# A weight load cut by partitions: three down-weight transfers of a routed expert layer issued as 112 + 8 + 8 partitions

## The chip, the cores and the metric

The kernel runs on one core of a Trainium2 chip. The metric is the device time of one launch in microseconds. The kernel before takes 1207.47 us, the median of three runs (1206.26 to 1207.69). One further execution was profiled; all rows of a trace below come from it.

## The reference, cut to what matters

One decoder layer over 256 tokens of width 1024: a layer norm, two token mixers, then an expert layer with 32 experts of which each token uses four. Only the expert layer touches the change. Each expert has up weights of 1024 x 2048 floats (8 MB) and down weights of 1024 x 1024 floats (4 MB).

```python
def expert_block(args):
    e, tok = args
    xe = x[tok]
    gu = xe @ w_up[e] + b_up[e]
    g = jnp.minimum(gu[:, :F], SWIGLU_LIMIT)
    u = jnp.clip(gu[:, F:], -SWIGLU_LIMIT, SWIGLU_LIMIT)
    act = (u + 1.0) * (g * jax.nn.sigmoid(SWIGLU_ALPHA * g))
    return act @ w_down[e] + b_down[e]
```

The results are weighted by the router's gates, added up per token, added to the residual and normalised again.

## The kernel before

The first part of the kernel (up to about 320 us) does the mixers and the router. After it the experts are worked through one after another, at 32 *positions*: position 0 to 31 is an order of the experts that is found at run time from the number of tokens each one has. All experts' weights have to be read from HBM, 384 MB in all.

Weights live in a ring of five buffers, `R[0]` to `R[4]`, of 128 partitions x 32 KB (4 MB) each. In the order listing they are R_67 to R_70 and R_1960. A position needs three buffers' worth: the first half of the up weights ("a"), the second half ("b") and the down weights ("d"). For positions 5 to 29 (`WHOLE`, line 28) one transfer fills a whole buffer; positions 30 and 31 and the early ones are loaded in halves of 2 MB, and the very last half is cut into four pieces of 128 partitions x 4 KB (lines 208 to 210).

`load_next` (line 177) issues one load on SyncE's queue as soon as a buffer is released. `free(p, k)` calls it right behind the last matmul that reads a half buffer. The list `order` (line 167) says what is loaded next: a, b of a position, and the down weights of the position before between them. The address of an expert is read into a register first (line 190).

In a down load, `src` is the expert's down matrix seen as 128 partitions x 2 halves x 4096 floats, that is, two runs of 16 KB for each partition, and `to` is the same shape in the ring. Each load completes on one of eight semaphores (DMAHW0 to DMAHW7 in the order listing), which are used in turn. Every engine that takes part in a load ends its share with a packet of 4 bytes to that semaphore. Behind position 17's up weights `load_row` (line 843) also loads one row of 4 KB into a single partition, issued at 796.84 us.

`step` (line 957) is the work of a position on TensorE: `up_part` for the up matmuls (line 703) and `down_half` for the down matmuls (line 730). The first matmul that reads a buffer waits for its load. TensorE's order of work around the change is written out by hand (`steps`, line 159, and the loop at line 1097). Behind position 31 come the scatter (line 745), the statistics (lines 1131 to 1137), a loop over left-over tokens that has nothing to do in this run (line 1154), the last normalisation (lines 1200 and 1204) and the stores (line 1205).

Of the kernel before, what the change touches and what calls it, by code (L numbers as in the profile page):

```python
# [27 lines left out]
WHOLE = range(5, 30)  # L28
LEFT_AT, RESIDUAL_AT, NORM_AT = 5, (7, 12), 17
W0, W1, W2, W3, W4, W5 = 9, 3, 9, 7, 5, 3  # L30
MS = {mybir.EngineType.PE}
STARTS = {mybir.EngineType.PE, mybir.EngineType.DVE, mybir.EngineType.Activation}

# [21 lines left out]
def tile_kernel(ctx: ExitStack, tc: tile.TileContext, x, ln_in_g, ln_in_b, w_in, gmlp_ln_g, gmlp_ln_b,  # L55
                w_spatial, b_spatial, w_branch_a, w_branch_b, w_out, ln_mix_g, ln_mix_b, w_router,
                b_router, w_up, b_up, w_down, b_down, ln_ffn_g, ln_ffn_b, out):
    nc = tc.nc
# [7 lines left out]
    def ps_mm():  # L66
        return bank["pool"].tile([P, 512], FT, name="mm", bufs=bank["mm"])
# [104 lines left out]
    def half(slot):  # L172
        return R[slot // 2][:, slot % 2 * 4096:slot % 2 * 4096 + 4096]
# [3 lines left out]
    def load_next(slot):  # L177
        done.append(slot)
        if len(ring) == len(order):
            return  # L180
        p, k = order[len(ring)]
        n = 2 if p in WHOLE else 1
        if len(done) < n:
            return
        slots = done[-n:]
        done.clear()
        for i, to in enumerate(slots):
            ring[p, k[0] + str(int(k[1]) + i)] = to
        if p not in expert_at:
            expert_at[p] = nc.values_load(dyn["ids"][0:1, p:p + 1], engines=[mybir.EngineType.SP], min_val=0,  # L190
                                          max_val=NE - 1)
        e, h = expert_at[p], int(k[1])
        if n == 2:
            assert h == 0 and slots[0] % 2 == 0 and slots[1] == slots[0] + 1
            to = R[slots[0] // 2]
        else:
            to = half(slot)
        if k[0] == "d":
            src = wd[e] if isinstance(e, int) else wd[bass.ds(e, 1)].rearrange("o p h n -> (o p) h n")
            if n == 2:  # L200
                to = to.rearrange("p (h n) -> p h n", h=2)
            else:
                src = src[:, h]
        else:
            src = wu[e] if isinstance(e, int) else wu[bass.ds(e, 1)].rearrange("o p n -> (o p) n")
            lo = 8192 * (k[0] == "b") + 4096 * h
            src = src[:, lo:lo + 4096 * n]
        if len(ring) == len(order):
            for j in range(4):
                nc.sync.dma_start(to[:, j * 1024:(j + 1) * 1024], src[:, j * 1024:(j + 1) * 1024])  # L210
        else:
            nc.sync.dma_start(to, src)

# [352 lines left out]
    for i in range(n_pieces):  # L566
# [29 lines left out]
        if nm == "A" and hf == 1:  # L596
            attend()
            for slot in (4, 5, 6, 7):
                load_next(slot)
        if nm == "B":  # L600
            to_T(G1, hTh, hTl, (hf,))
        if i >= n_pieces - 3:
            for slot in ((2, 3), (0,), (1,))[i - n_pieces + 3]:
                load_next(slot)
# [30 lines left out]
    sp2 = ctx.enter_context(tc.tile_pool(name="s2", bufs=1, reuse_waits="tile"))  # L635
    R.append(sp2.tile([P, 8192], FT, name="R4"))
    load_next(8)
    load_next(9)
    hT2 = sp2.tile([P, NC, 2 * GRP * CAP], FT, name="hT2")
# [439 lines left out]

    with tc.manual_schedule(engines=MS):  # L1080
        def free(p, k):
            load_next(ring[p, k])
# [71 lines left out]
    with tc.For_i(0, n_left) as i:  # L1154
# [27 lines left out]
        for j in range(2):  # L1182
            to = [ps_mm(), ps_mm()]
# [51 lines left out]
```

## Time and profile before

| | us |
|---|---|
| median of three runs | 1207.47 |
| lowest, highest | 1206.26, 1207.69 |
| the profiled execution | 1209.77 |
| its span, first to last instruction | 1208.0 |
| TensorE busy in the span | 1111.3 |
| VectorE busy | 414.3 |
| ScalarE busy | 214.8 |
| GpSimd busy | 110.9 |
| moved by DMA | 451.06 MB |

The profiled execution lies 2.3 us above the median, and 1.8 us of it lie outside the span. Times on the rows count from the span's start. The core has 16 DMA engines that carry all transfers; "DMA share" is how busy they are on average, so that 0.50 may be eight engines working and eight with nothing left. A transfer is split over the engines in packets, here one for each contiguous run.

### The profile page before, as it was taken

How to read it: one execution, taken by the hardware profiler on the slowest of the kernel's cores; microseconds unless marked ns; L12 is line 12 of the kernel's file. 1: busy time of each engine (PE TensorE's matmuls, PEld its weight loads, DVE VectorE, ACT ScalarE, POOL GpSimd, SP SyncE). 2: the span in 40 equal slices, each digit the busy share in tenths (PEclk: the TensorE clock that was granted, in tenths of full speed). 3: DMA queues.
4: the chain of work that ended last, by engine and by line, in shares of the span. 5: the costliest groups of instructions: out<-in, count | busy, mean ns of one | idle time of the engine just before them, and what ended most of it. 6: DMA issues, size and time to landing. Idle time of an engine off the chain costs nothing. (4 is left out here: it accounts for less than half of the span.)

```text
span 1208.0 us, 21799 instructions
## 1 busy us (share of the span) xinstructions
PE 1111.3 (92%) x9725; PEld 581.6 (48%) x9725; DVE 414.3 (34%) x787; ACT 214.8 (18%) x355; POOL 110.9 (9%) x121
## 2 busy tenths in 40 slices
PE   8999999999899889889999998999999899999793
PEld 6787888874444244343444343434333434344331
DVE  7964645564413123113122231413222221222213
ACT  5445643422101001010000010101010100010010
POOL 2800200000000001001000000100010010100000
PEclk8999999999999889788999999899999999999886
DMA  9554548667899999999999999999999999999993
GB/s 350 196 209 159 223 175 312 245 261 296 356 430 431 430 430 432 436 425 432 426 435 430 431 434 429 428 399 431 431 432 431 432 431 431 430 431 429 428 429 132
DMA packets 44208, 451.06 MB, mean 373 GB/s; under 512 B 2968, under 2 KB 3628, under 8 KB 26064
## 3 DMA queue, kind: packets, MB, share of 16 engines
q1 hardware_dynamic: 43504, 449.47, 88.8%
q8 instruction: 78, 1.28, 0.4%
q10 hardware_dynamic: 608, 0.16, 0.1%
q14 instruction: 18, 0.15, 0.0%
HBM read 448.58 MB, written 1.05 MB: 372 GB/s over the span
## 5 line engine op out<-in xcount | busy, mean ns | idle before, releaser
L703 PE MATMUL mm<-R,hT 128*32 128x512 f32 x3136 | 374.8, 603 | 5.3 <-DMA R<-in_w_up_dram 5.3
L730 PE MATMUL at<-R,actT 128*32 128x256 f32 x3328 | 222.6, 410 | 19.9 <-DMA R<-in_w_down_dram 10.8
L703 PEld LDWEIGHTS mm<-R,hT 128*32 128x32 f32 x3136 | 89.1, 110 | 185.0 <-issue 171.0
L709 DVE TENSOR_SCALAR gg<-mm 64x512 f32<-64x512 f32 x49 | 33.5, 683 | 380.2 <-PE mm L703 380.1
L730 PEld LDWEIGHTS at<-R,actT 128*32 128x32 f32 x3328 | 102.5, 116 | 116.0 <-issue 35.0
L712 POOL TENSOR_TENSOR gg<-gg,sg 64x512 f32<-64x512 f32 x52 | 66.0, 1270 | 842.0 <-ACT sg L710 842.0
L480 DVE TENSOR_TENSOR wlo<-R,whi 128x1024 fp32r<-128x1024 f32 x80 | 112.2, 1415 | 77.6 <-ACT whi L472 77.2
L530 PE MATMUL mm<-whi,hTh 128*128 128x512 f32 x256 | 100.7, 401 | 0.8 <-ACT R L489 0.8
L530 PE MATMUL mm<-wlo,hTh 128*128 128x512 f32 x256 | 99.9, 398 | 0.3 <-DVE wlo L480 0.3
L530 PE MATMUL mm<-whi,hTl 128*128 128x512 f32 x256 | 99.9, 398 | 0.0
L472 ACT ACTIVATE whi<-R 128x1024 fp32r<-128x1024 f32 x80 | 84.3, 1056 | 86.8 <-PE mm L530 80.9
L710 ACT ACTIVATE sg<-gg 64x512 f32<-64x512 f32 x52 | 32.8, 631 | 282.5 <-DVE gg L709 260.4
L737 ACT ACTIVATE y<-at 128x256 f32<-128x256 f32 x52 | 20.0, 384 | 342.5 <-PE at L730 342.5
L662 PEld LDWEIGHTS tp<-pt,xn 128*128 128x128 f32 x448 | 57.6, 201 | 29.5 <-DVE hT L667 18.8
L662 PE MATMUL tp<-pt,xn 128*128 128x128 f32 (+2 forms) x448 | 67.4, 296 | 0.0
L745 PE MATMUL ac<-y,qt 32*128 32x256 f32 x832 | 61.5, 410 | 0.5 <-ACT y L737 0.5
L670 ACT ACTIVATE hT<-tp,lm 128x128 f32<-128x128 f32 (+2 forms) x56 | 24.9, 444 | 182.2 <-PE tp L662 182.2
L745 PEld LDWEIGHTS ac<-y,qt 32*128 32x128 f32 x832 | 38.6, 189 | 37.6 <-issue 34.8
L722 DVE COPY actT<-tp 128x256 f32<-128x256 f32 x52 | 22.1, 425 | 95.3 <-PE tp L720 95.2
L720 PEld LDWEIGHTS tp<-ident,act 64*128 64x128 f32 x208 | 28.8, 209 | 54.0 <-issue 18.7
L530 PEld LDWEIGHTS mm<-wlo,hTh 128*128 128x128 f32 x256 | 48.0, 188 | 12.6 <-DVE wlo L480 1.4
L530 PEld LDWEIGHTS mm<-whi,hTh 128*128 128x128 f32 x256 | 48.2, 189 | 11.9 <-ACT R L489 0.9
(273 smaller groups left out, 844.8 us busy)
## 6 DMA issues: line engine op xcount, KB each, us to landing
R<-in_w_up_dram SPq DMA_DIRECT2D x50, 4096.0 KB, 29.3
R<-in_w_down_dram SPq DMA_DIRECT2D x25, 4096.0 KB, 29.1
R<-in_w_up_dram SPq DMA_DIRECT2D x28, 2048.0 KB, 11.5
R<-in_w_in_dram SPq DMA_DIRECT2D x13, 2048.0 KB, 11.7
R<-in_w_down_dram SPq DMA_DIRECT2D x13, 2048.0 KB, 33.0
R<-in_w_branch_a_dram SPq DMA_DIRECT2D x2, 2048.0 KB
R<-in_w_branch_b_dram SPq DMA_DIRECT2D x2, 2048.0 KB, 8.8
R<-in_w_out_dram SPq DMA_DIRECT2D x2, 2048.0 KB
```

The costliest lines, as they stand in the source:

```text
L472: nc.scalar.activation(hi, w, AF.Copy)
L480: nc.vector.tensor_tensor(lo, w, hi.bitcast(FT), op=OP.subtract)
L530: nc.tensor.matmul(ps[t], (a_l if k == 1 else a_h)[:, c, t * P:(t + 1) * P], (lo if k == 2 else hi)[:, cc], start=c == 0 and k == 0, stop= ...
L662: nc.tensor.matmul(ps[:, i * w:(i + 1) * w], zn[:, t, c * P:(c + 1) * P], pt[:, t, :w], start=t == 0, stop=t == T - 1)
L670: nc.scalar.activation(dst[:, c, :w], ps[:, i * w:(i + 1) * w], AF.Identity, scale=lm[:, 0, c:c + 1], bias=lm[:, 1, c:c + 1])
L703: nc.tensor.matmul(ps[n * CAP:(n + 1) * CAP], xs[:, c], w[:, o:o + 512], start=False, stop=c == NC - 1)
L709: nc.vector.tensor_scalar(gg, ps[:2 * CAP], LIMIT, None, op0=OP.min)
L710: nc.scalar.activation(sg, gg, AF.Sigmoid, scale=SW_ALPHA)
L712: nc.gpsimd.tensor_tensor(gg, gg, sg, op=OP.mult)
L720: nc.tensor.transpose(ps[:, c * 2 * CAP:(c + 1) * 2 * CAP], v[:, c], ident[:2 * CAP, :2 * CAP])
L730: nc.tensor.matmul(py[n * CAP:(n + 1) * CAP, :256], at[:, c, h], w[:, o:o + 256], start=h == 0 and c == 0, stop=h == 1 and c == 3)
L745: nc.tensor.matmul(to[n // 2][:, n % 2, t * 256:(t + 1) * 256], qt[s, t], y[s], start=start and t == 0, stop=stop and t == T - 1)
```

## The change

At positions 27, 28 and 29 the down load of 128 partitions becomes three loads on the same queue, one behind another: partitions 0 to 111, 112 to 119 and 120 to 127. The bytes, their places and their order are the same.

```diff
+EIGHTHS = (27, 28, 29)
...
         if len(ring) == len(order):
             for j in range(4):
                 nc.sync.dma_start(to[:, j * 1024:(j + 1) * 1024], src[:, j * 1024:(j + 1) * 1024])
+        elif k[0] == "d" and p in EIGHTHS:
+            for lo, hi in ((0, 112), (112, 120), (120, 128)):
+                nc.sync.dma_start(to[lo:hi], src[lo:hi])
         else:
             nc.sync.dma_start(to, src)
```

SyncE's queue at position 29, before: the down load into R_1960, then the two halves of position 30's "b". The brackets name the semaphores that an issue waits for; PE is TensorE's.

```order
L212 DMA R_1960<-in_w_down_dram 128x2x4096 [waits DMAHW7_49,PE_49]
L212 ISA
L212 DMA R_70<-in_w_up_dram 128x4096 [waits DMAHW0_49,PE_49]
L212 ISA
L212 DMA R_70<-in_w_up_dram 128x4096 [waits PE_49]
```

The same place with the change (line 212 is now 214 or 216):

```order
L214 DMA R_1960<-in_w_down_dram 112x2x4096 [waits DMAHW1_49,PE_49]
L214 ISA
L214 DMA R_1960<-in_w_down_dram 8x2x4096 [waits DMAHW2_49]
L214 ISA
L214 DMA R_1960<-in_w_down_dram 8x2x4096 [waits DMAHW3_49]
L216 ISA
L216 DMA R_70<-in_w_up_dram 128x4096 [waits DMAHW4_49,PE_49]
L216 ISA
L216 DMA R_70<-in_w_up_dram 128x4096 [waits DMAHW5_49,PE_49]
```

Two issues were added, each with its own semaphore and a wait for the load that used that semaphore last; what follows stands two places later in the queue and completes on other semaphores.

TensorE's queue at the down matmuls of position 29 (two blocks of tokens, 64 matmuls), up to the first up matmul of position 30's "b"; before:

```order
L685 MATMUL tp<-ident,ptg 128x128
L730 MATMUL at<-R_1960,actT 32x256 [waits DMAHW5_49]
L730 MATMUL at<-R_1960,actT 32x256 x31
L730 MATMUL at<-R_1960,actT 32x256 [waits Activation_49]
L730 MATMUL at<-R_1960,actT 32x256 x15
L745 MATMUL ac<-y,qt 128x256 x8
L730 MATMUL at<-R_1960,actT 32x256 x16
L703 MATMUL mm<-R_70,hT_1963 32x512 [waits DMAHW6_49]
```

With the change:

```order
L689 MATMUL tp<-ident,ptg 128x128
L734 MATMUL at<-R_1960,actT 32x256 [waits DMAHW3_49,DMAHW2_49,DMAHW1_49]
L734 MATMUL at<-R_1960,actT 32x256 x31
L734 MATMUL at<-R_1960,actT 32x256 [waits Activation_49]
L734 MATMUL at<-R_1960,actT 32x256 x15
L749 MATMUL ac<-y,qt 128x256 x8
L734 MATMUL at<-R_1960,actT 32x256 x16
L707 MATMUL mm<-R_70,hT_1963 32x512 [waits DMAHW4_49]
```

No matmul has moved. The first of position 29 waits for three loads in place of one, and so do those of positions 27 and 28.

## Rows read from the trace of the kernel before

**Rows 1.** The page, section 2: forty slices of 30.2 us each.

```profile
PE   8999999999899889889999998999999899999793
...
DMA  9554548667899999999999999999999999999993
GB/s 350 196 209 159 223 175 312 245 261 296 356 430 431 430 430 432 436 425 432 426 435 430 431 434 429 428 399 431 431 432 431 432 431 431 430 431 429 428 429 132
```

**Rows 2.** Busy time by stretch; last columns granted clock, DMA share, GB/s.

```profile
core 0: us, PE busy (x) PEld busy (x) DVE busy (x) ACT busy (x) POOL busy (x), PEclk, DMA share, GB/s
440.00:1180.00 740.00, 682.17 (x6928) 293.96 (x6924) 180.26 (x408) 65.52 (x134) 54.62 (x43) 0.95 1.00 429
1050.00:1100.00 50.00, 47.23 (x532) 21.82 (x536) 13.28 (x30) 4.63 (x10) 3.72 (x3) 1.00 1.00 429
1181.00:1182.00 1.00, 0.48 (x5) 0.31 (x3) 0.42 (x1) 0.08 (x1) 0.00 (x0) 1.00 0.90 377
1182.00:1183.00 1.00, 1.00 (x18) 0.72 (x16) 0.42 (x1) 0.00 (x0) 0.00 (x0) 1.00 0.50 205
1186.00:1187.00 1.00, 0.64 (x8) 0.16 (x8) 0.00 (x0) 0.00 (x0) 0.00 (x0) 1.00 0.51 209
1187.00:1188.00 1.00, 0.63 (x8) 0.16 (x8) 0.00 (x0) 0.00 (x0) 0.00 (x0) 1.00 0.35 131
1188.00:1189.00 1.00, 0.01 (x2) 0.00 (x0) 0.00 (x0) 0.00 (x0) 0.00 (x0) 1.00 0.00 0
```

**Rows 3.** What TensorE waited for, 440 to 1200 us: total, times, longest.

```profile
PE at L730 <- DMA R<-in_w_down_dram: 8.8, 5, 3.7
...
PE mm L703 <- DMA R<-in_w_up_dram: 1.7, 1, 1.7
```

**Rows 4.** Timeline of TensorE, 1090 to 1190 us: two waits for weights.

```profile
1119.86 1.92 PE L703 MATMUL mm<-R,hT 128*32 128x512 f32 x16 [1.70 <-DMA R<-in_w_up_dram]
...
1139.33 6.46 PE L730 MATMUL at<-R,actT 128*32 128x256 f32 x64 [3.65 <-DMA R<-in_w_down_dram]
```

**Rows 5.** Timeline of all engines from 1185 us to the end.

```profile
1187.37 0.64 PE L730 MATMUL at<-R,actT 128*32 128x256 f32 x8 [0.63 <-DMA R<-in_w_down_dram]
...
1189.43 1.08 PE L730 MATMUL at<-R,actT 128*32 128x256 f32 x8 [1.42 <-DMA R<-in_w_down_dram]
...
1191.01 2.09 PE L745 MATMUL ac<-y,qt 32*128 32x256 f32 x16 [0.50 <-ACT y L737]
...
1199.19 0.75 DVE L1200 SCALAR_TENSOR_TENSOR R<-ac,f_mv,R 128x512 f32<-128x512 f32 x1 [2.32 <-issue]
...
1200.76 4.68 SPq L1205 DMA_DIRECT2D out_dram<-R  x4
```

**Rows 6.** SyncE's issues, 1040 to 1170 us: start, length, transfers.

```profile
1048.12 0.38 SPq L212 DMA_DIRECT2D R<-in_w_down_dram  x1
...
1083.04 0.38 SPq L212 DMA_DIRECT2D R<-in_w_down_dram  x1
...
1104.18 0.38 SPq L212 DMA_DIRECT2D R<-in_w_down_dram  x1
...
1130.73 17.90 SPq L212 DMA_DIRECT2D R<-in_w_down_dram  x3
1149.94 14.41 SPq L210 DMA_DIRECT2D R<-in_w_down_dram  x4
```

**Rows 7.** Issue to landing of positions 27 and 29, from two windows.

```profile
R<-in_w_down_dram SPq DMA_DIRECT2D x1, 4096.0 KB, 32.6
...
R<-in_w_down_dram SPq DMA_DIRECT2D x1, 4096.0 KB, 35.1
```

**Rows 8.** What SyncE waited for, 1100 to 1190 us: total, times, longest.

```profile
SPq L210 <- DMA R<-in_w_up_dram: 12.6, 4, 4.4
...
SPq L212 <- DMA R<-in_w_down_dram: 8.1, 1, 8.1
```

**Rows 9.** The load of the experts' down biases: its line, then its packets.

```profile
L1043 SPq DMA_DIRECT2D tables<-in_b_down_dram x1: 422/422/422, 267.6 to 267.6; - x1
...
DMA packets 50, 0.12 MB, mean 216 GB/s; under 512 B 21, under 2 KB 21, under 8 KB 50
...
q1 hardware_dynamic: 50, 0.12, 54.9%
```

**Rows 10.** The same load by stretch, columns as in rows 2.

```profile
277.90:278.45 0.55, 0.55 (x9) 0.32 (x6) 0.01 (x1) 0.00 (x0) 0.00 (x0) 1.00 0.55 216
278.10:278.30 0.20, 0.20 (x4) 0.10 (x1) 0.00 (x0) 0.00 (x0) 0.00 (x0) 1.00 0.83 328
```

**Rows 11.** Packets of 812.6 to 813.7 us, then of 814.2 to 814.7 us.

```profile
DMA packets 34, 0.53 MB, mean 480 GB/s; under 512 B 12, under 2 KB 12, under 8 KB 13
...
DMA packets 16, 0.36 MB, mean 721 GB/s; under 512 B 5, under 2 KB 5, under 8 KB 5
```

## The prediction

> **What bounds the kernel now.** I read the page's slices first. From the twelfth slice on the DMA row stands at 9 and the GB/s row at about 430 (399 once), up to the last slice, while TensorE is busy for nine tenths as well [rows 1]. The stretch table puts numbers on it: from 440 to 1180 us the DMA share is 1.00 at 429 GB/s, and TensorE is busy for 682 of 740 us [rows 2]. Both are full, so I asked which waits for which. TensorE waited for weights 10.5 us in all after 440 us, but the waits that count lie late: 1.70 us before an up matmul at 1119.86, 3.65 us before position 29's down matmuls at 1139.33, and then for the last pieces, up to the last eight down matmuls at 1189.43 [rows 3 to 5]. The loads are issued far ahead: position 27's down weights land 32.6 us after their issue at 1048.12, position 29's 35.1 us after 1104.18, and the last four pieces are issued by 1164.4 but used up to 1189.43 [rows 5 to 7]. So the queue never runs dry at the end: the end is the time at which the DMA engines have carried everything, plus a tail of 18.6 us (1189.43 to 1208.0) in which nothing is loaded.
>
> The reader should look at how the transfers end. The share is 0.90 in 1181 to 1182, then 0.50 in 1182 to 1183 and still 0.51 in 1186 to 1187, at 205 and 209 GB/s, 0.35 in the next us, and then nothing [rows 2]. Half of the sixteen engines have run out of work at about 1182 (0.90 is half an engine set for the whole us and the other half for 0.8 of it), the other half goes on to about 1188 (the last packet lies a little behind 1187.7, which the mean share gives). All loads before are split evenly, so one half has fallen some 6 us behind the other. I call them the early and the late half.
>
> **The change, part by part.** No instruction of a compute engine is added or moved; TensorE's three first down matmuls wait for three loads in place of one, that is, for the last of them. What changes is six more issues on SyncE and which DMA engine carries which partition.
>
> *The issues.* One takes 0.38 us with its address [rows 6], so 0.4 to 0.8 us a position, hidden by the 30 us between issue and landing. Each also waits for the load that used its semaphore last, eight loads before. Such waits exist already: the last pieces waited 12.6 us for up loads that way [rows 8]. With three loads for one, eight loads in flight hold less: around position 29 the three pieces, the four halves of position 30's first two loads and one whole load, 16 MB, which is 39 us of transfer at 429 GB/s. I cost this at nothing; without that cover it would be 0.8 us a position.
>
> *The 112 partitions.* At 429 GB/s an engine carries 26.8 GB/s, so a partition's row of 32,768 bytes takes 1.22 us, and a down load is eight rows an engine, 9.78 us. 112 rows over sixteen engines are seven rows each, 8.56 us: 1.22 us less on all sixteen.
>
> *The two pieces of eight partitions.* Eight partitions split evenly over eight engines are one row each; two such pieces give one set of eight engines two more rows: 9 against 7. No row shows a transfer of eight partitions with long rows, nor which engines take it, so this is the term to bound. [...]
>
> From below: the eight engines run at their own pace, 1.22 us a piece. From above: the rate goes with the partitions written; full speed is only ever seen here with 128 of them, 3.35 GB/s each, so eight get 26.8 GB/s and a piece of 262,144 bytes takes 9.78 us. The nearest row lies between: the down biases are loaded into 32 partitions in rows of 4 KB, and in the 0.55 us in which nothing else starts 216 GB/s are reached, 328 GB/s in the best 0.2 us [rows 9, 10]. That is more than a quarter of 429 GB/s (107), so the upper bound is not the whole truth, but in no part is it the full rate either. Scaled to eight partitions, 216 gives 54 GB/s and 4.85 us a piece; 328 gives 82 GB/s and 3.2 us. I take 4.85, the mean, because the 0.2 us moved only 64 KB, a quarter of one piece, and a short burst says little of what can be kept up; the mean contains the start and end of the burst, so it errs to the slow side.
>
> [...]
>
> *The sum.* A position costs the eight engines 8.56 + 2 x 4.85 = 18.26 us instead of 9.78: 8.48 us more, and 25.4 us at three positions. If they are the early half, it ends at 1182 + 25.4 = 1207.4 instead of 1182, while the late half, three rows lighter, ends at 1188 - 3.7 = 1184.3. The last transfer moves from 1188 to 1207.4: 19.4 us. The late landings at positions 27 to 29 come before TensorE's work there and make it wait, with no slack left at position 29 [rows 4]; those waits are the same delay met earlier, not another one. The tail is unchanged. On the profiled execution (1209.77 us; span 1208.0) that gives 1229.2; it lies 2.3 us above the median, so I forecast 1226.9, say 1227 us.
>
> The bounds of the same sum: with 3.2 us a piece, 8.56 + 6.4 - 9.78 = 5.2 a position, the early half ends at 1197.5 and the kernel loses 9.5 us; with 9.78 a piece it loses 49. Other engines that write to the same partitions would be held up too; that lifts the cost above 19 and is the reason for the upper end of my range.
>
> **The rivals.**
>
> *A: eight engines at full pace, and they are the early half.* Then the early half gains three rows: 1182 + 3.7 = 1185.7; the late half loses three: 1184.3. The end moves from 1188 to 1185.7, at most 2.3 us; as the engines of a half do not end together (the share falls to 0.90 and 0.35 in the stretches in which they end, not at once), I count 1.3 us: 1206.2 us. For it: in the 32-partition load a packet of 4 KB still took 0.167 us on its engine (54.9% of 16 engines for 0.55 us, over 29 packets that are not ends of 4 bytes), 24.6 of the 26.8 GB/s [rows 9], and the one load of a single partition among the weights was carried by an engine that was early: its packet of 4 KB lies where eleven engines (twelve ends less its own) had finished the load before it, and the other five did so 0.5 to 2 us later [rows 11]. Against it: nothing of that size was ever sent to few partitions. It decides if a piece takes under 1.6 us: from 8.56 + 2 x 1.6 - 9.78 = 2.0 us more a position, the early half ends at 1188 or behind it.
>
> *B: full pace, but the late half takes the pieces.* It ends at 1188 + 3.7: 1211.1 us. For it: no row shows which engines take eight partitions. Against it: the single-partition load went to an early engine, which was to be had in eleven of sixteen cases by accident [rows 11].
>
> *C: the pieces are spread over all sixteen engines, so that nothing is balanced.* Same bytes an engine, 1207.5 us. Against it: eight rows do not divide among sixteen unless the two runs of a row are parted.
>
> **How the numbers follow.** Forecast (the eight engines share what few partitions take): 0.55, with its own range 1216 to 1245. A: 0.29. B: 0.07. C: 0.05. The rest, 0.04, is slower by something not named. About 0.2% (2.4 us) is what a measurement of this kernel tells from no change. A gives faster beyond that in a quarter of its cases, 0.07; the rest of A and C are within it, 0.27; the forecast, B and the rest are slower, 0.66. The range takes in A on one side and most of the forecast's upper part on the other: 1205 to 1243, which leaves out some 0.12, nearly all of it above.
>
> **What would show it.** Right: in the stretch table the DMA rate falls well below 429 GB/s for several us at three places between 1070 and 1150, with TensorE waiting 5 to 10 us before the down matmuls of positions 27 to 29, and the last down matmul starts near 1209. Right in the balance but wrong in the price (A): the rate stays at 430 and the stretch at half rate before the end shrinks from 6 us to 1 or 2. B: it grows to about 13 us. Wrong altogether: TensorE's waits late in the program grow although the rate stays at 430, which would put the cost on SyncE's semaphores.

## The result: 1277 to 1305 us, slower by 6.2%, and the profile after

The changed kernel takes 1294.0 us in the median against 1207.1 us for the kernel before on the same chip; the ratio is 1.0623 [1.0592, 1.0653]. The loss is 87 us by the median of all four runs, while the ratio stands for a loss of 76 us, as it counts the two faster runs (1277.1 and 1288.2 us) alone. Either is about four times the 19.4 us that were forecast, and all four runs lie above the range. The changed kernel's runs lie far apart (1277 to 1305 us), and so do those of 112 and 16 partitions below (1266 to 1283 us); the kernel before stays within 6 us in every comparison. The profiled execution, with a span of 1303.1 us, is the longest of the four; its span is 95 us above the 1208.0 us of before.

The page's slices of the changed kernel (32.6 us each here) answer to [rows 1]:

```profile
PE   8999999999998898989999899999989993534293
...
DMA  9556458569999999999999999999999999999991
GB/s 351 198 182 226 158 178 360 215 264 361 426 435 427 431 433 434 433 431 428 429 431 435 424 433 431 431 434 433 429 431 427 430 327 200 235 226 193 265 379 51
```

Up to the 32nd slice the rate is that of before. From the 33rd on the DMA row still stands at 9, but the rate falls, to 327 GB/s and then to about half (193 to 265) for five slices. The DMA engines are as busy as ever, and each byte takes twice as long. The stretches, with the columns of [rows 2], put it in numbers:

```profile
core 0: us, PE busy (x) PEld busy (x) DVE busy (x) ACT busy (x) POOL busy (x), PEclk, DMA share, GB/s
440.00:1060.00 620.00, 576.82 (x5882) 250.52 (x5878) 156.17 (x360) 55.01 (x114) 45.73 (x36) 0.96 1.01 431
1060.00:1240.00 180.00, 80.80 (x749) 30.98 (x742) 19.12 (x40) 6.14 (x13) 6.32 (x5) 0.72 1.00 224
1130.00:1140.00 10.00, 0.00 (x0) 0.00 (x0) 0.88 (x2) 0.00 (x0) 0.41 (x1) 0.55 1.01 154
1240.00:1250.00 10.00, 9.50 (x148) 4.80 (x144) 0.00 (x0) 0.77 (x2) 0.00 (x0) 0.99 1.00 424
1265.00:1270.00 5.00, 5.00 (x46) 1.63 (x42) 0.85 (x2) 0.00 (x0) 0.00 (x0) 1.00 0.54 221
1270.00:1275.00 5.00, 3.04 (x44) 1.07 (x36) 2.06 (x3) 0.63 (x1) 1.25 (x1) 1.00 0.13 53
1285.00:1286.00 1.00, 0.39 (x12) 0.03 (x4) 0.00 (x0) 0.00 (x0) 0.00 (x0) 1.00 0.03 12
1286.00:1287.00 1.00, 0.61 (x8) 0.13 (x8) 0.00 (x0) 0.32 (x1) 0.00 (x0) 1.00 0.00 0
```

From 1060 to 1240 us the share is 1.00 and the rate 224 GB/s, where 429 were moved before. At 429 GB/s the same bytes would have taken 180 x 224 / 429 = 94 us, so 86 us are lost there. The rest is lost at the end: the share is 0.54 from 1265 us, 0.13 (as much as two engines of sixteen) from 1270 us, and reaches zero at 1286 us. Before, the engines ran out over 7 us (1181 to 1188); now it takes over 20.

TensorE feels it as waits, here from 1060 us on (engine, what it waited for, total, times, longest), against [rows 3]; then the wait before position 27's down matmuls on TensorE's timeline, and from the page the median time from issue to landing of the three 112-partition loads, against [rows 7]:

```profile
PE mm L707 <- DMA R<-in_w_up_dram: 53.8, 6, 20.4
PE at L734 <- DMA R<-in_w_down_dram: 43.1, 7, 15.4
```

```profile
1109.13 6.03 PE L734 MATMUL at<-R,actT 128*32 128x256 f32 x64 [14.06 <-DMA R<-in_w_down_dram]
```

```profile
R<-in_w_down_dram SPq DMA_DIRECT2D x3, 3584.0 KB, 60.8
```

The two waits are 96.9 us together. From 1060 us on the kernel before had 6.0 us of such waits at the down matmuls and 1.7 at the up matmuls, so 89 us are new, nearly all of the 95 by which the span is longer. The larger one is for up weights, and each of their loads goes into 128 partitions as before: the change delays loads that it does not touch. The granted clock is 0.55 in the mean at 1130 to 1140 us and 0.50 at 1140 to 1150, and TensorE does nothing there. Behind such a wait, the 64 matmuls at 1109.13 took 6.03 us at a granted clock of 0.60, where the same 64 took 3.66 us (at 1090.43, clock 1.00) in the kernel before. That is small beside the waits: TensorE is busy for 1116.0 us in all, against 1111.3 before.

### The profile page after: what moved, and what is told of

Same layout as the page of the kernel before. It is cut to its first block, busy times and chain, and to the rows that moved or that the text cites. A ratio compares the mean times of both kernels' runs of the same rounds, so it can differ in the third digit from the quotient of the medians.

```text
span 1303.1 us, 21822 instructions
## 1 busy us (share of the span) xinstructions
PE 1116.0 (86%) x9725; PEld 578.7 (44%) x9725; DVE 412.1 (32%) x787; ACT 214.8 (16%) x355; POOL 110.0 (8%) x121
## 2 busy tenths in 40 slices
DMA packets 44256, 451.06 MB, mean 346 GB/s; under 512 B 3016, under 2 KB 3676, under 8 KB 26112
## 5 line engine op out<-in xcount | busy, mean ns | idle before, releaser
L707 PE MATMUL mm<-R,hT 128*32 128x512 f32 x3136 | 384.6, 617 | 57.4 <-DMA R<-in_w_up_dram 57.4
L666 PEld LDWEIGHTS tp<-pt,xn 128*128 128x128 f32 x448 | 56.6, 198 | 29.1 <-DVE hT L671 18.8
```

Source lines behind the costliest of these rows:

```text
L666: nc.tensor.matmul(ps[:, i * w:(i + 1) * w], zn[:, t, c * P:(c + 1) * P], pt[:, t, :w], start=t == 0, stop=t == T - 1)
L707: nc.tensor.matmul(ps[n * CAP:(n + 1) * CAP], xs[:, c], w[:, o:o + 512], start=False, stop=c == NC - 1)
```

## The experiments

All change only how the down weights of positions 27 to 29 are loaded, that is, the loop over the three parts. Kernels that leave weights out are compared by the moment at which their last load ends, since TensorE then hides part of the loss (with none of the three loads, the last load ends at 1162 us of a span of 1191.5). That moment is read from the stretch in which the GB/s column reaches zero: 1188 us before [rows 2], 1286 us for the changed kernel. It comes from one execution of each kernel.

**Three transfers, all of 128 partitions.** This keeps the three issues and semaphores and splits the columns in place of the partitions.

```diff
-for lo, hi in ((0, 112), (112, 120), (120, 128)):
-    nc.sync.dma_start(to[lo:hi], src[lo:hi])
+for h, lo, hi in ((0, 0, 4096), (1, 0, 2048), (1, 2048, 4096)):
+    nc.sync.dma_start(to[:, h, lo:hi], src[:, h, lo:hi])
```

> Positions 27 to 29 load their down weights in three transfers, cut by columns (16 KB, 8 KB and 8 KB of each of the 128 partitions) instead of by partitions. Theory P (the two pieces of eight partitions are dear) and theory Q (the 112-partition load itself is dear): 1207 us, within 2 us of the kernel before, because every transfer still has 128 partitions. Theory S (six more issues and their semaphores are dear): near the changed kernel, 1280 to 1300 us.

Measured: 1208.2 us, 1.000 [0.9991, 1.001]. Three transfers for one cost nothing, as the prediction had it. The loss lies in the choice of partitions.

**The 112 partitions alone**, and **the two pieces alone**:

```diff
+nc.sync.dma_start(to[:112], src[:112])            # only112
...
+for lo, hi in ((112, 120), (120, 128)):           # only8s
+    nc.sync.dma_start(to[lo:hi], src[lo:hi])
```

> Positions 27 to 29 load partitions 0 to 111 alone; partitions 112 to 127 keep what an earlier load left there, so the output is not the reference's. Theory P: 16 partitions less to carry and no pieces, 1200 to 1207 us, and the DMA rate stays at 430 GB/s. Theory Q: 1235 to 1260 us, and the rate falls to 150 to 300 GB/s from position 27 on as in the changed kernel.

> Positions 27 to 29 load partitions 112 to 119 and 120 to 127 alone, in the two pieces; partitions 0 to 111 keep what an earlier load left, so the output is not the reference's. 21 rows an engine fewer are carried than before (25.6 us of transfer). Theory P with the 4.85 us a piece of the forecast: the two pieces take 9.7 us on their engines, as long as the whole load did, so 1200 to 1207 us; if the pieces alone carry the loss of 87 us, 1260 us or more. Theory Q: the pieces go at a cost of a few us, 1185 to 1200 us (TensorE sets the end then).

Measured: 1260.5 us for the 112 partitions alone, 1.0439 [1.0381, 1.0497], and 1213.8 us for the pieces alone, 1.0052 [1.0032, 1.0072]. As a base for both, **none of the three loads**:

```diff
+pass                                              # none
```

> Positions 27 to 29 load no down weights at all (TensorE multiplies with what an earlier load left; the output is not the reference's). It is the floor for the kernels that load the pieces alone: 12 MB or 29 us of transfer less than before, so TensorE sets the end. Both theories: 1190 to 1203 us, the DMA rate at 430 GB/s whenever the engines are busy.

Measured: 1191.0 us, 0.9858 [0.9796, 0.9919]. The 112 partitions alone lie at the top of what theory Q gave them, with runs of 1254.5 and 1266.5 us. The pieces alone miss every range given for them: 1200 to 1207 us by P, 1260 or more if they carry the whole loss, 1185 to 1200 by Q. The stretches of the three, in the order none, only112, only8s (columns as above):

```profile
1161.00:1162.00 1.00, 1.00 (x12) 0.71 (x12) 0.12 (x1) 0.00 (x0) 0.00 (x0) 1.00 0.25 102
1162.00:1163.00 1.00, 1.00 (x10) 0.20 (x2) 0.30 (x1) 0.00 (x0) 0.00 (x0) 1.00 0.00 0
```

```profile
1070.00:1080.00 10.00, 7.95 (x78) 2.49 (x68) 3.60 (x6) 1.26 (x2) 2.14 (x2) 1.00 1.06 205
...
1246.00:1247.00 1.00, 0.38 (x12) 0.06 (x8) 0.00 (x0) 0.00 (x0) 0.00 (x0) 1.00 0.02 8
1247.00:1248.00 1.00, 0.58 (x8) 0.10 (x8) 0.00 (x0) 0.35 (x1) 0.00 (x0) 1.00 0.00 0
```

```profile
1066.00:1068.00 2.00, 2.00 (x28) 1.35 (x24) 0.31 (x1) 0.44 (x1) 0.00 (x0) 1.00 0.99 123
1068.00:1070.00 2.00, 1.50 (x32) 0.67 (x28) 0.41 (x1) 0.40 (x2) 0.00 (x0) 1.00 1.03 131
...
1194.00:1195.00 1.00, 0.59 (x8) 0.11 (x8) 0.00 (x0) 0.00 (x0) 0.00 (x0) 1.00 0.04 16
1195.00:1196.00 1.00, 0.64 (x8) 0.16 (x8) 0.00 (x0) 0.08 (x1) 0.00 (x0) 1.00 0.00 0
```

The last load ends at 1162 us without the three loads, at 1247 us with 112 partitions each, at 1195 us with the pieces. The 112 partitions, 11.0 MB in all, would take 26 us at 429 GB/s and took 85: 59 us lost. The pieces, 1.6 MB, would take 4 and took 33: 29 us lost. Together 88 us, of the 98 by which the changed kernel's last load is late. The other 10 are less than the 28 us by which its runs differ, so they say nothing.

How many engines take a transfer can be counted, as each ends its share with a packet of 4 bytes. The pages of none, only112 and only8s:

```profile
DMA packets 43392, 438.48 MB, mean 368 GB/s; under 512 B 2920, under 2 KB 3580, under 8 KB 26016
```

```profile
DMA packets 44112, 449.49 MB, mean 355 GB/s; under 512 B 2968, under 2 KB 3628, under 8 KB 26064
```

```profile
DMA packets 43536, 440.05 MB, mean 363 GB/s; under 512 B 2968, under 2 KB 3628, under 8 KB 26064
```

Three loads of 112 partitions add 48 packets under 512 bytes, sixteen engines each. Six pieces add 48 as well, eight engines each.

The pieces also show who pays. At 123 and 131 GB/s with a share of 1.0, the eight engines that have no part in a piece cannot be at full pace: they alone would carry half of 429, 214 GB/s. The trace has the size and the time of every packet and shows the same. Ten packets of up loads (32,768 bytes each) start in these 4 us; they took 3.7 to 4.5 us, where such a packet takes 1.21 us in the kernel before. The bystanders are held up as well.

The 112 partitions do the same to the loads beside them. From 1062 to 1095 us of only112, the packets of the down load (16,384 bytes) took 1.24 us in the median where 0.61 is usual, and those of the up loads in flight 2.47 us where 1.21 is usual. The stretch:

```profile
1060.00:1095.00 35.00, 24.94 (x253) 10.40 (x251) 8.25 (x17) 2.95 (x6) 2.52 (x2) 0.90 1.01 206
```

In these 35 us 7.2 MB were moved, about twice the 3.7 MB of one load of 112 partitions. So that load's own bytes are only half of the price. At 206 GB/s the 11.0 MB of three loads take 53 us, 28 more than at 429 GB/s; most of the rest of the 59 us is lost by up weights that go at half pace beside them.

**The same pieces spread over other partitions.** The rows are those of 112 to 127; they land in other partitions than the matmuls assume.

```diff
+for at, lo, hi in ((0, 112, 120), (8, 120, 128)):     # only8spread
+    nc.sync.dma_start(to[at:128:16], src[lo:hi])
...
+for at, lo, hi in ((0, 112, 120), (32, 120, 128)):    # only8even; only8odd: 64 and 96
+    nc.sync.dma_start(to[at:at + 32:4], src[lo:hi])
```

> As the kernel with the two pieces alone, the same source rows and bytes, but each piece is written to every sixteenth partition (0, 16, ... 112 and 8, 24, ... 120) instead of eight neighbours; the output is not the reference's. If eight neighbouring partitions as a destination are what makes a piece dear, the pieces take less than with neighbours, about 2.4 us each or less, and the time is lower than that of the two pieces alone if that one is above 1195 us. If it is the source rows or the eight engines, both kernels take the same time.

> As the two pieces alone, same source rows and bytes, but a piece is written to every fourth partition of 0 to 31 (the second of 32 to 63); the output is not the reference's. [...] Theory N (what counts is only how few partitions a load has): as the two pieces of neighbours, 1214 us and packets of 4 us.

> As the kernel before this one, but every fourth partition of 64 to 95 and of 96 to 127; the output is not the reference's. [...] Theory N: 1214 us as with neighbours. [...]

Measured: every 16th partition 1204.7 us, 0.9974 [0.9964, 0.9984]; every fourth of 0 to 63 1193.95 us, 0.9882 [0.9841, 0.9923]; every fourth of 64 to 127 1202.0 us, 0.996 [0.9933, 0.9987]. First the stretches of every fourth of 0 to 63, then of every fourth of 64 to 127:

```profile
1060.00:1070.00 10.00, 9.50 (x112) 5.74 (x108) 2.28 (x7) 2.21 (x5) 0.00 (x0) 1.00 1.00 429
...
1166.00:1167.00 1.00, 1.00 (x27) 0.60 (x20) 0.97 (x2) 0.57 (x1) 0.00 (x0) 1.00 0.00 0
```

```profile
1060.00:1070.00 10.00, 10.00 (x102) 5.12 (x95) 3.20 (x10) 1.37 (x3) 0.00 (x0) 1.00 1.00 310
...
1183.00:1184.00 1.00, 0.50 (x12) 0.06 (x4) 0.00 (x0) 0.38 (x1) 0.00 (x0) 1.00 0.00 0
```

Same rows read, same bytes, same issues, and the last load ends at 1166, 1183 or 1195 us, depending on the partitions that are written. In 0 to 63 the pieces run at 429 GB/s and cost 4 us, what their bytes take. In 64 to 127, as regularly spread, they cost 21 us; every 16th partition lies between the extremes in time. So eight partitions are not slow in themselves: the price of the same pieces goes from 4 us (every fourth partition of 0 to 63) to 33 us (neighbours, 112 to 127). Theory N, 1214 us for both, misses both, by 20 and 12 us.

**Other splits of all 128 partitions**, everything loaded and computed:

```diff
+for lo, hi in ((0, 64), (64, 128)):                   # s64_64
+for lo, hi in ((0, 112), (112, 128)):                 # s112_16
+    nc.sync.dma_start(to[lo:hi], src[lo:hi])
...
+for j in range(2):                                    # stride2
+    nc.sync.dma_start(to[j:128:2], src[j:128:2])
```

> Positions 27 to 29 load their down weights in two transfers, partitions 0 to 63 and 64 to 127, everything is computed. All sixteen engines carry the same number of rows. [...] If it is only the uneven or the very narrow loads that cost: 1207 us.

> Loads of positions 27 to 29 as two transfers: partitions 0 to 111 and 112 to 127. [...] Rival R2 (the number of small transfers or the engines left out of them sets the price): sixteen engines share the rows evenly, nothing is left out of step, 1255 to 1264 us.

> Loads of positions 27 to 29 as two transfers of every second partition each (0, 2, ..., 126 and 1, 3, ..., 127). [...]

Measured: 64 and 64 neighbours 1256.1 us, 1.0396 [1.0351, 1.0441]; 112 and 16 1277.4 us, 1.0593 [1.0558, 1.0627]; every second partition 1208.3 us, 1.000 [0.999, 1.001]. The stretch at 1070 us of 64 and 64, then of every second:

```profile
1070.00:1080.00 10.00, 9.50 (x136) 5.22 (x136) 0.42 (x2) 1.22 (x3) 0.00 (x0) 1.00 0.98 208
```

```profile
1070.00:1080.00 10.00, 9.50 (x137) 4.91 (x136) 0.82 (x2) 1.68 (x4) 0.00 (x0) 1.00 1.07 457
```

If only uneven or very narrow loads cost, 64 and 64 would have taken 1207 us; it is neither, and 1256.1 were measured. Rival R2 gave 112 and 16 partitions 1255 to 1264 us and misses too: no engine is left out of its transfers (3016 packets under 512 bytes against 2920 with none of the loads: 96 ends for six transfers, sixteen each), and it takes 1277.4 us. Nor does the number of partitions decide: 64 neighbours run at half pace (208 GB/s), 64 as every second one at full pace (457 GB/s). As the slow and the fast kernel of this pair differ in the rows read as well, the next two part reads from writes.

**Reads of the one, writes of the other:**

```diff
+    nc.sync.dma_start(to[j:128:2], src[64 * j:64 * j + 64])     # dst2, j = 0, 1
+    nc.sync.dma_start(to[64 * j:64 * j + 64], src[j:128:2])     # src2
```

> Two transfers a position as in the run with every second partition, but with the rows 0 to 63 of the weights read into the even partitions and the rows 64 to 127 into the odd ones (the rows land in other partitions than the matmuls assume, the bytes are the same). Theory T (the partitions written decide): full pace as with every second partition, 1205 to 1211 us, 430 GB/s at 1070 to 1080. Rival U (the rows read from HBM decide, 64 neighbouring rows read by sixteen engines at once): 1245 to 1262 us, 205 to 230 GB/s.

> The reverse: the even rows of the weights are read into partitions 0 to 63 and the odd rows into 64 to 127 (again the rows land in other partitions than the matmuls assume). Theory T (the partitions written decide): slow as partitions 0 to 63 and 64 to 127 were, 1245 to 1262 us, 205 to 230 GB/s at 1070 to 1080. Rival U (the rows read decide): full pace, 1205 to 1211 us, 430 GB/s.

Measured: 1208.0 us, 1.0001 [0.9991, 1.0011], with neighbouring rows written to every second partition; 1266.9 us, 1.0504 [1.0447, 1.0561], with every second row written to neighbouring partitions, a little above the 1262 that theory T gave. The same stretch of each:

```profile
1070.00:1080.00 10.00, 10.00 (x140) 4.54 (x136) 0.00 (x0) 0.38 (x1) 0.00 (x0) 1.00 1.04 446
```

```profile
1070.00:1080.00 10.00, 10.00 (x135) 4.37 (x130) 0.00 (x0) 0.38 (x1) 0.00 (x0) 1.00 1.02 218
```

The partitions written decide (208 and 218 GB/s for 64 neighbours, 457 and 446 for every second one), the rows read from HBM don't. Rival U, that of the reads, is out.

**One position alone.**

```diff
-EIGHTHS = (27, 28, 29)
+EIGHTHS = (27,)          # p27; p29: (29,)
```

> Only position 27 is loaded in three transfers, 28 and 29 in one each. Theory G: each position pays its own price, a third of 87 us: 1232 to 1242 us, with the rate below 260 GB/s for one stretch of 20 to 40 us from 1060 us and about 430 before and behind it. Rival S (once out of step, the engines stay so, and later whole loads are slow too): over 1250 us, with the rate well below 430 GB/s after 1110 us.

> Only position 29 is loaded in three transfers, 27 and 28 in one each. Theory G: as for position 27 alone, 1232 to 1242 us, since nothing is loaded behind the last pieces that could make up for it. Rival S (the delay lasts as long as loads follow): less than at position 27, as fewer loads follow, 1215 to 1230 us.

Measured: position 27 alone 1227.9 us, 1.0179 [1.0156, 1.0202], a little under the 1232 of theory G (each position pays its own price); position 29 alone 1232.7 us, 1.0207 [1.018, 1.0234], within G's range. The stretches of position 27 alone:

```profile
1080.00:1090.00 10.00, 8.22 (x65) 2.90 (x54) 7.21 (x15) 1.26 (x2) 2.55 (x2) 1.00 1.01 174
1090.00:1100.00 10.00, 0.00 (x0) 0.00 (x0) 0.23 (x1) 0.00 (x0) 0.00 (x0) 0.63 1.01 283
1100.00:1110.00 10.00, 9.11 (x108) 4.54 (x112) 0.00 (x0) 0.38 (x1) 0.00 (x0) 0.69 1.00 429
```

At 1100 us the rate is back at 429 GB/s. So rival S falls: the disturbance ends with its own loads, and position 29, with fewer loads behind it, costs 25 us against 20. Three times 20 to 25 is 60 to 75; the changed kernel's runs lose 70 to 98, so it is not shown whether three close together cost more than three apart.

No run beat the kernel before with all weights loaded; the fast splits only equal it.

## Why the prediction was wrong, step by step

**The step that failed is the term "The 112 partitions".** It gave seven rows an engine at 1.22 us a row, so 8.56 us a load, "1.22 us less on all sixteen", a gain of 3.7 us over three positions. Measured alone, the three loads lost 59 us: 85 us for what would take 26. The row of 1.22 us came from loads of 128 partitions, and I carried it to 112 partitions without bounds, while I bounded only the eight-partition pieces. The 112-partition load had no row in the trace either. A split of 64 and 64, with no small piece in it at all, loses 48 us. The term was wrong twice: the load's own packets took twice their usual time (1.24 us against 0.61), which is about half of the 59 us, and the up loads in flight went at half pace with them (2.47 us against 1.21), for which the sum had no term.

**The price of the pieces came out near, in part by luck.** That eight engines carry a piece, with which the sum counts, had no row of before; only8s shows it (48 ends for six pieces). That the two pieces of a position go to the same eight, and that these are the early half, no run shows. The forecast had 4.85 us a piece; an engine's row in a piece is two packets, which took about 2 us each, so some 4 us. But the forecast charged the pieces to eight engines, with 6 us of slack to use up first, and they cost all sixteen: 123 GB/s at a share of 1.0. Alone they moved the last load by 33 us. That this is near the forecast's 29.1 us for six pieces is luck, as those were the work of eight engines and not a delay of all. The prediction named that other engines "would be held up too" as a reason for the upper end; it should have been in the sum. It also spoke only of engines that write to the same partitions, whereas the loads held up here go to all 128.

**The issues** at nothing: right (cols3, 1.000). **The direction** and the kind of cause (the pace depends on which partitions are written): right. **The rivals** A, B and C all rested on full pace and are out, C also by the count of eight engines a piece; only8even shows that A's premise, eight partitions at full pace, can hold, for partitions that are spread over 0 to 63 (429 GB/s). The rival that was missing is one in which the large part slows down.

**The balance of the two halves**, on which the sum was built, did not decide: with such a load in flight no half is at full pace, as all sixteen engines together move 123 GB/s (pieces alone) or 206 (112 partitions alone), less than the 214 of one half. The signs named beforehand came in kind, and in size beyond it: the rate fell not for several us at three places but for 180 us with hardly a gap, TensorE waited up to 20.4 us and not 5 to 10, and more for up weights (53.8 us) than for down weights (43.1).

What the trace of before could have told: 429 GB/s is the rate of loads of 128 partitions [rows 2], and none of the rows that I read has a large transfer with fewer. The 112 partitions were as untried a shape as the pieces and needed bounds as they did.

**What stays open** is why the partitions written set the pace: 429 against 310 GB/s for pieces in 0 to 63 and in 64 to 127, half pace for 112 and 64 neighbouring partitions (205 and 208 GB/s), full pace for every second partition (457). How rows are dealt to engines in transfers of fewer than 128 partitions is not shown; the views count the engines but do not number them.

## What to carry to other kernels

Don't carry the pace of a full-height load over to a load of fewer partitions: 112 or 64 neighbouring partitions ran at half of it (205 and 208 GB/s against 429), and so did the up loads in flight with the 112 (packets of 2.47 us against 1.21). Where a load has to be split, split columns, or take every second partition (both 1.000 here). A DMA share of 1.00 says that the engines are occupied, not that they move bytes (here it stood beside 429 GB/s and beside 224); read it beside GB/s.

## What the runs showed of the hardware

- Loads of 112 and of 64 neighbouring partitions run at half pace: 205 and 208 GB/s, against 420 to 457 for 128 partitions and for every second one. The writes decide (446 against 218 GB/s with reads exchanged).
- A load of few neighbouring partitions slowed the loads in flight beside it: pieces of eight neighbouring partitions (112 to 127), on eight engines, took all sixteen down to 123 GB/s, and packets of other loads to 3.7 to 4.5 us from 1.21. By what path other engines are held up no run shows.
- The disturbance is gone as soon as its loads are: 429 GB/s from 1100 us on, with position 27 alone.
- Two of the slow splits scatter in time: 1277 to 1305 us (the changed kernel) and 1266 to 1283 us (112 and 16), where the kernel before keeps within 6 us. Why was not tried.
